# A two-layer decoder on one Trainium2 core: half-size parcels of filler in the stick-breaking mixer, one PSUM bank for two products of a down part, and weight parts behind the copy of u

## The chip, the cores and the metric

The kernel runs on one core of one Trainium2 chip. The metric is the device time of one execution in microseconds (us), as the median over runs. Times of single instructions come from one execution that the hardware profiler recorded. In what follows PE is TensorE (matrix products), PEld its weight load, ACT is ScalarE, DVE is VectorE, POOL is GpSimd and SP is SyncE, which issues nearly all transfers here. PSUM is the memory that PE writes its products to; it has eight banks, each of 512 fp32 columns on 128 partitions.

## The reference

The kernel computes two layers of a decoder for one sequence of 512 tokens with 1024 features. Each layer adds three things to the residual stream x: half a SwiGLU feed-forward (FFN), a mixer, and half a second FFN. The mixer of layer 0 is a gated linear attention (GLA), that of layer 1 a stick-breaking attention (SB).

```python
def swiglu(h, w_gate, w_up, w_down):
    return (jax.nn.silu(h @ w_gate) * (h @ w_up)) @ w_down

def sb_mixer(h, w_in, w_out):
    ...
        z = jnp.einsum('bhtd,bhsd->bhts', q_blk, k).astype(jnp.float32) * scale
        ...
        sp = jnp.where(mask, jax.nn.softplus(z), 0.0)
        rem = lax.cumsum(sp, axis=3, reverse=True) - sp
        weights = jnp.where(mask, jnp.exp(jax.nn.log_sigmoid(z) - rem), 0.0)
        return jnp.einsum('bhts,bhsd->bhtd', weights.astype(v.dtype), v)
    ...
    return o @ w_out

def reference(x, ...):
    for i in range(DEPTH):                                  # DEPTH = 2
        x = x + 0.5 * swiglu(rmsnorm(x, ffn1_norm[i]), ...)  # d_ff = 2816
        h = rmsnorm(x, mix_norm[i])
        y = gla_mixer(h, ...) if i % 2 == 0 else sb_mixer(h, ...)
        x = x + y
        x = x + 0.5 * swiglu(rmsnorm(x, ffn2_norm[i]), ...)
    return rmsnorm(x, final_norm)
```

## The kernel before

**Products.** Every large product is made of three: an operand is cut into a high part (a cast, `wh` or `xh`) and a low part (the difference, `wl` or `xl`), and PE adds high by high, low by high and high by low into one PSUM bank (`mm3`, line 68). Cutting a weight costs ACT the cast of line 129 and DVE the difference of line 130. x stays on chip, feature-major (`xs`, eight tiles of 128 features by 512 tokens).

**The queue of work.** All weight work is a list of entries in `feed` (line 140). An entry has weight units and a body, a generator that issues matmuls and yields between parcels. `Feed.start` (line 144) begins an entry: it cuts the units of this entry and of the next two, as long as these hold no more than four large units (1024 elements a partition), looks one entry further for the sums of weights, and issues the transfers of six entries. Within an engine the program order is what is written, but a scheduler places the engines' instructions by priority; `tc.issue_after(x)` puts what is issued under it behind x. `feed.step(n)` (line 161) runs n parcels. A mixer calls it between its own operations, so that PE has filler while ACT and DVE work on the attention.

**Sizes of parcels.** `feat` (line 192) makes 128 features for 512 tokens in 24 matmuls of 512 columns, in two parcels. `tok` (line 211) makes 256 features token-major in 96 matmuls of 256 columns, in four parcels. `back` makes the projection back into x, and `two_halves` (line 561) takes the first two `feat` entries of a phase in turn.

**PSUM.** `psum` (line 47) hands out the eight banks in the order of "aazzztto", or by a tag.

**The FFN.** Most gate and up products are made by `seven` (line 666): a product of 2 x 2 blocks with seven block products in place of eight, as in Strassen's and Winograd's schemes. It queues two entries. `body_1` takes three weight units (a block, `sums_12`, two blocks) and makes the first four block products with 256 columns each: w, q, w again, z; ACT copies the first w into z (line 718). `body_2` takes one unit (`sums_34`) and makes the other three: w (12 matmuls, operand `t_half(2)`), then the copy of w to u on ACT (`u3`, line 736), then q, then w. Its adds and gates are on DVE (lines 737, 740, 706).

**Down parts.** `down` (line 300) adds one part of the down projection into x, with 512 columns a matmul. For two of the six groups of each FFN, `seven_down` (line 336) does it with seven block products: its entries are again a `body_1` and a `body_2`, sixteen pairs of them in the kernel. In `body_1` each of the two q products (m = 0, 1; six matmuls of 256 columns each) takes a bank of its own, and an add into x (line 378) follows each product. w and z take two banks each as well, so that one `seven_down` holds six.

**The SB mixer.** `SB` (line 1257) queues the input projections as filler: for each of eight pairs of heads a q and a k `feat` entry (`pair`), and four `tok` entries for v (`vals`); the projection back follows. `evac_k` (line 1296) turns one product into the two heads' keys: a multiplication by the norm (`n`), then two casts to `kh` (one on ACT, one on DVE) and two operations for `kl` of each head. `run` (line 1394) goes over 17 iterations s. Iteration s makes the logits and running sums of head s (`weights_log`: z on PE; four ACT operations; scans on DVE; r on DVE, line 1352) and the transposes and exponentials of head s-1 (`weights`: `ps_T` on PE, `wt` on ACT, line 586); after each odd head `values` (line 1373) multiplies by v for a pair (`ps_oT`, line 1381). Pair p is needed by iteration 2p, the values of group c by the iteration that closes pair 2c. How many parcels of filler each iteration gets is written out by hand:

```python
                steps = [3] * 12 + [2, 1, 1, 2, 2]
```

Of the kernel before, what the change touches and what calls it, by code (L numbers as in the profile page):

```python
# [21 lines left out]
KD = D // P  # L22
# [10 lines left out]
def decoder(ctx: ExitStack, tc: tile.TileContext, a: dict, out: bass.AP):  # L33
# [60 lines left out]
    class Entry:  # L94
# [4 lines left out]
        def __init__(self, units, body, place=0, lead=False):  # L99
            self.units, self.body, self.W, self.place = units, body, None, place  # L100
            self.lead, self.views = lead, None

# [5 lines left out]

        def split(self):
            if self.W is None:  # L110
                self.W = []
                for r, (_, _, n, m) in zip(self.view(), self.units):
                    few = n * m < 1024
# [26 lines left out]
    class Feed:  # L140
# [3 lines left out]
        def start(self):  # L144
            i = self.pos
            self.pos += 1
            used = 0
            for e in self.q[i : i + 3]:
                used += sum(n * m >= 1024 for _, _, n, m in e.units)
                if used > 4:  # L150
                    break
                e.split()
            for e in self.q[i : i + 4]:
                e.view()
            for e in self.q[i : i + 6]:
                for u in e.units:
                    u[0].load()
            e = self.q[i]
            return e.body(e.W)

        def step(self, n=1, end=None):
            while n > 0:
                if self.cur is None:
                    if self.pos == end:
                        return
                    self.cur = self.start()
                if next(self.cur, self) is self:
                    self.cur = None
                else:
                    n -= 1  # L170
# [21 lines left out]
    def feat(ch, f, evac, tag=None, defer=None):  # L192


        def body(W):
            (wh, wl), = W
            ps = psum("ps_f", tag)
            for part in (range(0, KD // 2), range(KD // 2, KD)):
                for k in part:
# [11 lines left out]
    def tok(w, c0, evac, tag=None):  # L211
# [3 lines left out]
        def body(W):  # L215
            ps = None
            for i in range(NT):
# [4 lines left out]
                for k in range(KD):  # L222
                    wh, wl = W[k // 4]
                    mm(o, st["h"][k][:, s], wh[:, k % 4], k == 0, False)
                    mm(o, st["h"][k][:, s], wl[:, k % 4], False, False)
                    mm(o, st["l"][k][:, s], wh[:, k % 4], False, k == KD - 1)
                if i % 2:
                    evac(i - 1, ps[:, 0:256])
                    evac(i, o)
# [6 lines left out]
    def back(w, r0, nf, hs, scale, nxt, late=0, tags=(None,) * 8):  # L236


        for dh in range(2):
# [27 lines left out]
            if nf == KD and late:  # L267

                def body(W, prod=prod, done=done):
                    for ms in ((0, 1), (2, 3)):  # L270
                        for f in range(nf - late):
                            for m in ms:
                                prod(W, f // 2, f % 2, m, f)
                            if f % 2:
                                yield
                    for m in range(4):
                        for f in range(nf - late, nf):
                            prod(W, f // 2, f % 2, m, f)
                        done(m)
                        yield  # L280

                feed.q.append(Entry([u for _, u in units], body))
                continue
            for f0, u in units:

                def body(W, f0=f0, prod=prod, done=done):
                    if f0 + 2 < nf:
                        for kk in range(2):
                            for m in range(4):
                                prod(W, 0, kk, m, f0 + kk)  # L290
                            yield
                    else:
                        for m in range(4):
                            for kk in range(2):
                                prod(W, 0, kk, m, f0 + kk)
                            done(m)
                            yield

# [37 lines left out]
    def seven_down(pool, w, r0, hs, part):  # L336
# [43 lines left out]
        def body_1(W):  # L380
# [5 lines left out]
            for m in range(2):  # L386
# [3 lines left out]
                nc.scalar.copy(zs[m], ws[m])  # L390
            yield
            for m in range(2):
                qs.append(psum("ps_q")[:, 0:H])
                prod(qs[m], s, 0, m, "t1", True)
                add(m, 1, 1, qs[m])
# [11 lines left out]
        def body_2(W):  # L407
# [9 lines left out]
            for m in range(2):  # L417
                prod(qs[m], s, 2, m, "b22", False)
                add(m, 0, 1, qs[m])
            yield  # L420
# [40 lines left out]
    st = {}  # L461
# [99 lines left out]
    def two_halves(between=None):  # L561
# [3 lines left out]
        for i in range(3):  # L565
            for x in g:
                next(x, None)
            if i == 0 and between is not None:
# [20 lines left out]
    class FFN:  # L589
# [76 lines left out]
        def seven(self, ch, group=None):  # L666
# [63 lines left out]
            def body_2(W):  # L730
# [4 lines left out]
                u3 = self.tp.tile([P, H], F32, tag="c", bufs=1, name="u3")  # L735
                nc.scalar.copy(u3, w)  # L736
                nc.vector.tensor_tensor(out=o1[:, H:T], in0=u3, in1=o1[:, H:T], op=ALU.add)
# [34 lines left out]
            feed.q.append(entry)  # L772
            feed.q.append(Entry([(ch, sums_34, KD, P)], body_2, NEAR))

        def t_half(self, i, j):
# [481 lines left out]
    class SB:  # L1257
# [5 lines left out]
        def __init__(self, w_in, w_out, nxt):  # L1263
# [11 lines left out]
            pair(0), vals(0), pair(1), pair(2), vals(1), pair(3), pair(4), vals(2)  # L1275
            pair(5), pair(6), vals(3), pair(7)
            back(w_out, 0, KD, self.hs, 1.0, nxt, late=2, tags=("a", "a", "z", "z", "z", "t", "t", "o"))
# [116 lines left out]
        def run(self):  # L1394
            with ExitStack() as es:
# [17 lines left out]
                feed.step(4)  # L1413
                steps = [3] * 12 + [2, 1, 1, 2, 2]
                for s in range(17):
# [3 lines left out]
                    if s < 16:  # L1419
                        for i, _ in enumerate(self.weights_log(p, e)):  # L1420
                            if i == 1:
                                feed.step(1)
                                n -= 1
                    if s > 0:
                        for i, _ in enumerate(self.weights(q, f)):
                            if i < 2 and n > 0:
                                feed.step(1)
                                n -= 1
                        feed.step(n)
                        if f == 1:  # L1430
                            self.values(q)
                    else:
                        feed.step(n)
                feed.entries(self.end + 2 - feed.pos)
# [321 lines left out]
```

## Time and profile before

| | us |
|---|---|
| three runs | 1831.89, 1834.36, 1835.29 |
| their median | 1834.36 |
| the profiled execution | 1833.41 |
| its span | 1831.5 |

By the tiles' names and times the phases lie about so: first FFN 23 to 345 us, GLA mixer to 585, FFN to 915, FFN to 1250, SB mixer to 1475, last FFN to the end.

A row of the page's first section gives an engine's busy time, its share of the span and its count of instructions. Rows of groups name line, engine, operation, output and inputs, shapes and count; behind the bar stand the busy time in us, the mean of one in ns, and the idle time of the engine before them with what ended it. In a list of waits stand the waiting product, what it waited for, the total, the count and the longest. In a timeline stand start, duration, and in brackets the idle time before. Matmuls overlap, so their pace is read from start to start; a matmul's shown duration is longer than its share of PE.

### The profile page before, as it was taken

Reading aid. Unit: us, or ns where it says so; the run is one execution under the profiler, and the core shown is the slowest. Engines: PE = TensorE matmul, PEld = TensorE weight load, DVE = VectorE, ACT = ScalarE, POOL = GpSimd, SP = SyncE. Lnnn points to the kernel's source line nnn. Section 1 sums busy time; section 2 is a strip of 40 time slices with the busy share of each in tenths; the row PEclk is TensorE's granted clock in tenths of the full one; section 3 lists DMA queues with packets and bytes.
Section 4 is the critical chain, followed back from the end, with each engine's and each line's share of the span. In section 5 each row is a group of like instructions: output and inputs, shape, how many; then the busy total and the mean of one; then the engine's idle time right before and its main releaser. Section 6 shows DMA issues by size and latency. Waiting matters only on the chain.

```text
span 1831.5 us, 30847 instructions
## 1 busy us (share of the span) xinstructions
PE 1820.1 (99%) x12496; PEld 1657.0 (90%) x12496; DVE 1544.3 (84%) x2529; ACT 1058.7 (58%) x1856; POOL 8.8 (0%) x20
## 2 busy tenths in 40 slices
PE   9999999999999999999999999999999999999998
PEld 7999999889888899999889999998888788999997
DVE  8999798676787989889798988976878779898886
ACT  6556555544555556555555555555878755565554
POOL 0000000000000000000000000000000000000000
PEclk9999999999999999999999999999999999999999
DMA  5433333221123333333333333322222133233331
GB/s 163 137 115 106 104 116 117 79 70 55 62 69 115 93 115 100 120 104 104 99 98 115 93 115 116 104 82 81 70 70 64 64 92 115 93 116 104 104 121 53
DMA packets 177794, 179.22 MB, mean 98 GB/s; under 512 B 4146, under 2 KB 168292, under 8 KB 177652
## 3 DMA queue, kind: packets, MB, share of 16 engines
q1 hardware_dynamic: 176800, 175.91, 30.8%
q8 instruction: 98, 1.61, 0.4%
q0 software_dynamic: 608, 1.05, 0.2%
q14 instruction: 44, 0.36, 0.1%
q10 hardware_dynamic: 244, 0.29, 0.0%
HBM read 175.17 MB, written 2.10 MB: 97 GB/s over the span
## 4 chain that ended last, share of the span: by engine, by line
PE 94%; DVE 4%; ACT 1%; DMA 1%; issue 0%; SPq 0%; DVEq 0%; ACTq 0%
PE ps_w L693 21%; PE ps_f L66 18%; PE ps_d L66 16%; PE ps_q L693 10%; PE ps_z L693 5%; PE ps_t L66 5%; PE ps_w L372 4%; PE ps_b L66 4%; PE ps_q L372 2%; PE ps_S L66 1%; PE ps_z L1319 1%; PE ps_z L372 1%; PE ps_oT L1381 1%; DVE wl L130 1%; PE ps_bt L66 1%; PE ps_T L1366 1%
## 5 line engine op out<-in xcount | busy, mean ns | idle before, releaser
L130 DVE TENSOR_TENSOR wl<-raw,wh 128x512 fp32r<-128x512 f32 (+1 forms) x242 | 256.7, 1061 | 66.8 <-ACT wh L129 47.7
L129 ACT CAST wh<-raw 128x512 fp32r<-128x512 f32 (+1 forms) x242 | 223.5, 925 | 97.7 <-PE ps_f L66 32.8
L130 DVE TENSOR_TENSOR wl<-s,wh 128x1024 fp32r<-128x1024 f32 x176 | 214.6, 1220 | 46.9 <-PE ps_z L693 29.1
L129 ACT CAST wh<-s 128x1024 fp32r<-128x1024 f32 x176 | 184.2, 1047 | 109.5 <-DVE s L683 25.1
L693 PE MATMUL ps_w<-th,wh 128*128 128x256 f32 x864 | 239.5, 277 | 1.0 <-ACT u L736 0.9
L693 PE MATMUL ps_w<-tl,wh 128*128 128x256 f32 x864 | 238.7, 276 | 0.0
L693 PE MATMUL ps_w<-th,wl 128*128 128x256 f32 x864 | 238.7, 276 | 0.0
L66 PE MATMUL ps_f<-xh,wh 128*128 128x512 f32 x432 | 172.4, 399 | 0.0
L66 PE MATMUL ps_f<-xl,wh 128*128 128x512 f32 x432 | 169.3, 392 | 0.0
L66 PE MATMUL ps_f<-xh,wl 128*128 128x512 f32 x432 | 168.9, 391 | 0.0
L693 PEld LDWEIGHTS ps_w<-th,wh 128*128 128x128 f32 x864 | 162.4, 188 | 1.8 <-ACT u L736 1.3
L66 PE MATMUL ps_d<-hh,wl 128*128 128x512 f32 x416 | 162.2, 390 | 0.0
L66 PE MATMUL ps_d<-hh,wh 128*128 128x512 f32 x416 | 162.2, 390 | 0.0
L693 PEld LDWEIGHTS ps_w<-th,wl 128*128 128x128 f32 x864 | 162.2, 188 | 0.0
L693 PEld LDWEIGHTS ps_w<-tl,wh 128*128 128x128 f32 x864 | 162.2, 188 | 0.0
L66 PE MATMUL ps_d<-hl,wh 128*128 128x512 f32 x416 | 161.8, 389 | 0.0
L129 ACT CAST wh<-rawd 128x1024 fp32r<-128x1024 f32 (+1 forms) x100 | 82.9, 846 | 71.8 <-issue 31.8
L130 DVE TENSOR_TENSOR wl<-rawd,wh 128x1024 fp32r<-128x1024 f32 (+1 forms) x100 | 96.0, 963 | 16.4 <-PE ps_z L693 8.6
L327 DVE SCALAR_TENSOR_TENSOR x<-ps_d,x 128x512 f32<-128x512 f32 x120 | 81.2, 686 | 22.9 <-PE ps_d L66 22.5
L66 PEld LDWEIGHTS ps_f<-xl,wh 128*128 128x128 f32 x432 | 81.1, 188 | 17.3
L66 PEld LDWEIGHTS ps_f<-xh,wl 128*128 128x128 f32 x432 | 81.3, 188 | 15.7
L66 PEld LDWEIGHTS ps_f<-xh,wh 128*128 128x128 f32 x432 | 81.2, 188 | 15.3
(353 smaller groups left out, 5286.1 us busy)
## 6 DMA issues: line engine op xcount, KB each, us to landing
raw<-in_ffn_w_gate_dram SPq DMA_DIRECT2D x43, 1024.0 KB, 5.4
raw<-in_ffn_w_up_dram SPq DMA_DIRECT2D x43, 1024.0 KB, 5.4
rawd<-in_ffn_w_down_dram SPq DMA_DIRECT2D x84, 512.0 KB, 3.6
raw<-in_gla_w_in_dram SPq DMA_DIRECT2D x12, 1024.0 KB, 5.3
raw<-in_sb_w_in_dram SPq DMA_DIRECT2D x16, 512.0 KB, 3.8
raw<-in_gla_w_out_dram SPq DMA_DIRECT2D x4, 1024.0 KB, 4.9
raw<-in_sb_w_in_dram SPq DMA_DIRECT2D x4, 1024.0 KB, 5.2
raw<-in_sb_w_out_dram SPq DMA_DIRECT2D x4, 1024.0 KB, 5.0
```

What stands on the lines that cost most here:

```text
L66: st["pe"] = nc.tensor.matmul(ps, l, r, start=first, stop=last).ins
L129: st["cut"] = nc.scalar.copy(h[:, k], part).ins
L130: nc.vector.tensor_tensor(out=l[:, k], in0=part, in1=h[:, k].bitcast(F32), op=ALU.subtract)
L327: nc.vector.scalar_tensor_tensor(out=xs[k], in0=ps, scalar=0.5, in1=xs[k], op0=ALU.mult, op1=ALU.add)
L372: st["pe"] = nc.tensor.matmul(ps, l_, r_, start=first and c + n == 0, stop=c == 1 and n == 2, skip_group_check=True).ins
L693: st["pe"] = nc.tensor.matmul(o, l_, r_, start=first and j + n == 0, stop=j == 3 and n == 2, skip_group_check=True).ins
L1319: nc.tensor.matmul(o_, l_, r_, start=first, stop=last, skip_group_check=True)
L1366: nc.tensor.transpose(ps[:, c0 : c0 + P], ys[yb][:, yc + j * P : yc + (j + 1) * P], ident)
L1381: nc.tensor.matmul(po[e * 64 : e * 64 + 64, j * P : T], self.v[j][:, c : c + 64], self.wt[p, e][bk][:, c0 : c0 + n], start=j == 0, stop=j ...
```

## The change

Three things change; the instructions are the same in number on every engine.

*Half-size parcels.* `feat` yields four times in place of two, `tok` eight times in place of four, the projection back twice where it did once. `Feed.step(n)` now runs 2n of these half parcels (`halves`), so that the GLA mixer keeps its sizes. The SB mixer hands them out itself: 6 half parcels in the first three iterations and 5 in the other fourteen, 88 in all as before. In its list of entries the last pair of heads goes ahead of the last group of values.

*One bank for two products.* In `seven_down` both q products go to the two halves of one PSUM bank. Only the first sets the start flag, and both adds follow both products, in `body_1` and in `body_2`.

*Weight parts behind the copy of u.* The `body_2` entries of `seven` are marked `mid`. Where such an entry starts, and the next entry is a down part, and the one behind that is another `seven` entry (or a `seven_down`; both have the place `NEAR`), only the first unit of that last entry is cut at once. The others (the sums `s12` and the two blocks) are cut after the first chunk of `body_2`, and issued behind the copy of u.

```diff
--- before.py
+++ after.py
@@ -98,7 +98,7 @@
 
         def __init__(self, units, body, place=0, lead=False):
             self.units, self.body, self.W, self.place = units, body, None, place
-            self.lead, self.views = lead, None
+            self.lead, self.views, self.mid = lead, None, False
 
         def view(self):
 
@@ -106,10 +106,13 @@
                 self.views = [view(ch.load()) for ch, view, _, _ in self.units]
             return self.views
 
-        def split(self):
+        def split(self, count=None, after=None):
             if self.W is None:
                 self.W = []
-                for r, (_, _, n, m) in zip(self.view(), self.units):
+            done = len(self.W)
+            with tc.issue_after(after) if after is not None else ExitStack():
+                for r, (_, _, n, m) in list(zip(self.view(), self.units))[done:count]:
                     few = n * m < 1024
                     if few:
 
@@ -145,20 +148,35 @@
             i = self.pos
             self.pos += 1
             used = 0
+            hold = None
+            if self.q[i].mid and i + 2 < len(self.q) and self.q[i + 1].units[0][0].few and self.q[i + 2].place == NEAR:
+                hold = self.q[i + 2]
             for e in self.q[i : i + 3]:
                 used += sum(n * m >= 1024 for _, _, n, m in e.units)
                 if used > 4:
+                    hold = None
                     break
-                e.split()
+                e.split(1 if e is hold else None)
             for e in self.q[i : i + 4]:
                 e.view()
             for e in self.q[i : i + 6]:
                 for u in e.units:
                     u[0].load()
             e = self.q[i]
-            return e.body(e.W)
+            return e.body(e.W) if hold is None else self.held(e, hold)
+        @staticmethod
+        def held(e, hold):
+            for n, _ in enumerate(e.body(e.W)):
+                if n == 0:
+                    hold.split(None, st["u3"])
+                yield
 
         def step(self, n=1, end=None):
+            self.halves(2 * n, end)
+        def halves(self, n, end=None):
             while n > 0:
                 if self.cur is None:
                     if self.pos == end:
@@ -195,7 +213,7 @@
         def body(W):
             (wh, wl), = W
             ps = psum("ps_f", tag)
-            for part in (range(0, KD // 2), range(KD // 2, KD)):
+            for part in (range(u, u + KD // 4) for u in range(0, KD, KD // 4)):
                 for k in part:
                     mm3(ps, wh[:, k], wl[:, k], st["h"][k], st["l"][k], k == 0, k == KD - 1)
                 if part[-1] == KD - 1:
@@ -224,6 +242,8 @@
                     mm(o, st["h"][k][:, s], wh[:, k % 4], k == 0, False)
                     mm(o, st["h"][k][:, s], wl[:, k % 4], False, False)
                     mm(o, st["l"][k][:, s], wh[:, k % 4], False, k == KD - 1)
+                    if k == KD // 2 - 1:
+                        yield
                 if i % 2:
                     evac(i - 1, ps[:, 0:256])
                     evac(i, o)
@@ -271,12 +291,12 @@
                         for f in range(nf - late):
                             for m in ms:
                                 prod(W, f // 2, f % 2, m, f)
-                            if f % 2:
-                                yield
+                            yield
                     for m in range(4):
                         for f in range(nf - late, nf):
                             prod(W, f // 2, f % 2, m, f)
                         done(m)
+                        yield
                         yield
 
                 feed.q.append(Entry([u for _, u in units], body))
@@ -289,11 +309,13 @@
                             for m in range(4):
                                 prod(W, 0, kk, m, f0 + kk)
                             yield
+                            yield
                     else:
                         for m in range(4):
                             for kk in range(2):
                                 prod(W, 0, kk, m, f0 + kk)
                             done(m)
+                            yield
                             yield
 
                 feed.q.append(Entry([u], body))
@@ -389,9 +411,12 @@
                 zs.append(psum("ps_z")[:, 0:H])
                 nc.scalar.copy(zs[m], ws[m])
             yield
+            ps = psum("ps_q")
             for m in range(2):
-                qs.append(psum("ps_q")[:, 0:H])
-                prod(qs[m], s, 0, m, "t1", True)
+                qs.append(ps[:, m * H : (m + 1) * H])
+                prod(qs[m], s, 0, m, "t1", m == 0)
+            for m in range(2):
                 add(m, 1, 1, qs[m])
             yield
             for m in range(2):
@@ -416,6 +441,7 @@
             yield
             for m in range(2):
                 prod(qs[m], s, 2, m, "b22", False)
+            for m in range(2):
                 add(m, 0, 1, qs[m])
             yield
             for m in range(2):
@@ -564,7 +590,7 @@
         g = [feed.start(), feed.start()]
         for i in range(3):
             for x in g:
-                next(x, None)
+                next(x, None), next(x, None)
             if i == 0 and between is not None:
                 between()
 
@@ -733,7 +759,7 @@
                 o0, o1 = v["o"]
                 prod(w, s, 0, lambda j: self.t_half(2, j), first=False)
                 u3 = self.tp.tile([P, H], F32, tag="c", bufs=1, name="u3")
-                nc.scalar.copy(u3, w)
+                st["u3"] = nc.scalar.copy(u3, w).ins
                 nc.vector.tensor_tensor(out=o1[:, H:T], in0=u3, in1=o1[:, H:T], op=ALU.add)
                 yield
                 prod(q, s, 4, half(4, 1), first=False)
@@ -771,6 +797,7 @@
             entry = Entry(units, body_1, NEAR, lead)
             feed.q.append(entry)
             feed.q.append(Entry([(ch, sums_34, KD, P)], body_2, NEAR))
+            feed.q[-1].mid = True
 
         def t_half(self, i, j):
 
@@ -1273,7 +1300,7 @@
                 tok(w_in, 2 * D + c * 256, lambda i, ps: self.evac_v(c, i, ps), "z" if c == 0 else "a")
 
             pair(0), vals(0), pair(1), pair(2), vals(1), pair(3), pair(4), vals(2)
-            pair(5), pair(6), vals(3), pair(7)
+            pair(5), pair(6), pair(7), vals(3)
             back(w_out, 0, KD, self.hs, 1.0, nxt, late=2, tags=("a", "a", "z", "z", "z", "t", "t", "o"))
 
         def evac_v(self, c, i, ps):
@@ -1411,7 +1438,8 @@
                 exp_ln_tables(st["sqrt"])
                 flush(self.defer)
                 feed.step(4)
-                steps = [3] * 12 + [2, 1, 1, 2, 2]
+                steps = [6] * 3 + [5] * 14
                 for s in range(17):
                     p, e = divmod(s, 2)
                     q, f = divmod(s - 1, 2)
@@ -1419,18 +1447,19 @@
                     if s < 16:
                         for i, _ in enumerate(self.weights_log(p, e)):
                             if i == 1:
-                                feed.step(1)
-                                n -= 1
+                                feed.halves(2)
+                                n -= 2
                     if s > 0:
                         for i, _ in enumerate(self.weights(q, f)):
-                            if i < 2 and n > 0:
-                                feed.step(1)
-                                n -= 1
-                        feed.step(n)
+                            if i < 2:
+                                k = min(n, n % 2 if i == 0 and n % 2 else 2)
+                                feed.halves(k)
+                                n -= k
+                        feed.halves(n)
                         if f == 1:
                             self.values(q)
                     else:
-                        feed.step(n)
+                        feed.halves(n)
                 feed.entries(self.end + 2 - feed.pos)
```

## The prediction

> **What bounds the kernel now.** I read the page first: its busy times and the granted clock.
>
> ```profile
> span 1831.5 us, 30847 instructions
> ...
> PE 1820.1 (99%) x12496; PEld 1657.0 (90%) x12496; DVE 1544.3 (84%) x2529; ACT 1058.7 (58%) x1856; POOL 8.8 (0%) x20
> ...
> PEclk9999999999999999999999999999999999999999
> ```
>
> TensorE (PE) is busy for all but 11.4 us of the span and its clock is granted in full. The change issues the same instructions as before on every engine, so it can save only time in which PE stands still or refills its pipeline. Next I asked which waits PE has; the columns are the total in us, the count and the longest.
>
> ```profile
> PE ps_q L372 <- DVE o L706: 1.1, 4, 0.3
> ...
> PE ps_w L693 <- ACT u L736: 0.9, 2, 0.7
> ...
> PE ps_z L1319 <- DVE r L1352: 0.4, 2, 0.2
> ...
> PE ps_oT L1381 <- ACT wt L586: 0.2, 1, 0.2
> ```
>
> Each of the three parts of the change meets one of these: the bank of the products of a down part (`ps_q` at line 372), the copy of u (line 736), and the mixer's filler (the last two). The waits of the first 23 us, left out here, are out of its reach. So the profile itself bounds the visible gain at 2.6 us; what a wait costs beyond its idle time comes next. Last I looked at the load of the other engines by stage: an FFN stretch, the mixer's regular part, and its tail.
>
> ```profile
> 1025.00:1050.00 25.00, 25.00 (x223) 25.00 (x223) 24.88 (x43) 15.69 (x28) 0.00 (x0) 1.00 0.37 116
> 1275.00:1425.00 150.00, 150.00 (x930) 122.81 (x928) 120.84 (x175) 124.29 (x249) 0.00 (x0) 1.00 0.22 68
> 1425.00:1450.00 25.00, 24.38 (x132) 16.90 (x131) 20.15 (x31) 22.08 (x49) 0.00 (x0) 1.00 0.13 43
> ```
>
> After the stretch's length stand the busy times of PE, its weight load, VectorE (DVE) and ScalarE (ACT). In the FFN, DVE is as full as PE; in the mixer ACT and DVE stand at 83% and 81%.
>
> **Part 1, one bank for two products.** The timeline of PE around one of the four waits, then around a place that the list of waits does not show:
>
> ```profile
> 254.20 0.28 PE L372 MATMUL ps_q<-hh,wl 128*128 128x256 f32 x1
> 254.31 0.28 PE L372 MATMUL ps_q<-hl,wh 128*128 128x256 f32 x1
> 254.88 0.38 PE L372 MATMUL ps_q<-hh,wh 128*128 128x256 f32 x1 [0.29 <-DVE o L706]
> 255.10 0.29 PE L372 MATMUL ps_q<-hh,wl 128*128 128x256 f32 x1
> ...
> 851.58 0.28 PE L372 MATMUL ps_q<-hl,wh 128*128 128x256 f32 x1
> 851.80 0.38 PE L372 MATMUL ps_q<-hh,wh 128*128 128x256 f32 x1
> ```
>
> Matmuls of this size start 0.113 us apart. Here the second q product starts 0.57 after its predecessor, and its next one 0.22 later: 0.46 + 0.11, so 0.56 us where the list shows 0.29 of idle time. A shown wait costs about twice its idle time. What it waits for is a gate of the unit before, which reads the bank that the product takes:
>
> ```profile
> 254.41 0.42 DVE L706 TENSOR_TENSOR o<-ps_w,o 128x256 f32<-128x256 f32 x1
> ```
>
> The gate ends at 254.83. With both q products in one bank the second takes no new bank, and a down part needs five of the eight instead of six; in the built order the gate's bank is reused after about 5 us of matmuls instead of 2.15. The four waits go: 4 x 0.56 = 2.24 us. At 851.80, and alike at 1762, 0.21 each goes too: 2.65 us in all.
>
> The price: the add of the first product (line 378) now follows both products, and PE may write the bank again (`b22`) only behind both adds.
>
> ```profile
> 139.35 0.75 DVE L378 SCALAR_TENSOR_TENSOR x<-ps_q,x 128x256 f32<-128x256 f32 x2
> ...
> 137.78 0.28 PE L372 MATMUL ps_q<-hl,wh 128*128 128x256 f32 x1
> ...
> 141.98 0.28 PE L372 MATMUL ps_q<-hh,wh 128*128 128x256 f32 x1
> ```
>
> The second product's last matmul starts at 137.78, the two adds end at 140.10 and the bank is written again at 141.98: 1.9 us of cover (PE's ws, zs and t3 products). The adds are behind both products already, since DVE's queue is late, so I take 0. The Trainium skill's page "PSUM — Partial Sum Buffer", section "PSUM bank collisions raise a hardware error", speaks against sharing: two engines may not touch one bank at once, so an add cannot run beside a product in the other half. By that rule the first add could move by six matmuls at most, an estimate of 0.68 us; the rows above show more cover than that.
>
> **Part 2, the weight parts behind the copy of u.** PE and then ACT around the longer of the two waits, and PE at the other:
>
> ```profile
> 661.36 0.28 PE L693 MATMUL ps_q<-nl,wh 128*128 128x256 f32 x1
> 662.29 0.39 PE L693 MATMUL ps_w<-th,wh 128*128 128x256 f32 x1 [0.66 <-ACT u L736]
> 662.52 0.28 PE L693 MATMUL ps_w<-th,wl 128*128 128x256 f32 x1
> ...
> 660.92 1.05 ACT L129 CAST wh<-s 128x1024 fp32r<-128x1024 f32 x1 [1.59 <-DVE s L677]
> 661.88 0.36 ACT L736 COPY u<-ps_w 128x256 f32<-128x256 f32 x1
> ...
> 1572.14 0.28 PE L693 MATMUL ps_q<-nl,wh 128*128 128x256 f32 x1
> 1572.66 0.38 PE L693 MATMUL ps_w<-th,wh 128*128 128x256 f32 x1 [0.24 <-ACT u L736]
> ```
>
> ACT's queue is in order. The cast of the down part's sums waits for DVE (the s of line 677) until 660.92 and holds the copy up until 661.88. PE's next product should have started at 661.47; it starts at 662.29 and refills for 0.11: 0.93 us. At 1572.66 it is 0.41 + 0.11 = 0.52. Both lie ahead of a down part, where the change puts the cast and its difference behind the copy: 1.45 us saved. The two moved pieces cost PE nothing if they are ready in time:
>
> ```profile
> L130 DVE TENSOR_TENSOR wl<-s,wh 128x1024 fp32r<-128x1024 f32 x176 | 214.6, 1220 | 46.9 <-PE ps_z L693 29.1
> L129 ACT CAST wh<-s 128x1024 fp32r<-128x1024 f32 x176 | 184.2, 1047 | 109.5 <-DVE s L683 25.1
> ```
>
> Cast and difference take 1.05 + 1.22 = 2.3 us. Between the copy and the first product of s lie two products of u's unit (24 matmuls, 2.7 us), the earlier down part (24 at twice the width, 5.4 us) and the products of a11 (12, 1.4 us): 9.5 us. What waits behind the copy's chunk on DVE is the rest of that unit's adds, which move at most by these 2.3 us. I take 0; bounds -0.3 to +1 us, since DVE is full there. A DMA that the swap of the mixer's parts moves three issues later on SP stays two raw buffers ahead: 0.
>
> **Part 3, half parcels.** The mixer's filler by groups, in 1275 to 1425:
>
> ```profile
> L66 PE MATMUL ps_f<-xh,wh 128*128 128x512 f32 x102 | 42.2, 414 | 0.0
> ...
> L66 PE MATMUL ps_t<-wh,xh 128*128 128x256 f32 x96 | 27.7, 288 | 0.0
> ...
> 1435.80 0.48 PE L66 MATMUL ps_b<-oh,wh 128*128 128x512 f32 x1
> ```
>
> A half parcel is 6 matmuls of 512 columns or 12 of 256: 12 x 0.113 = 1.36 us. With three matmuls a step the rows give 306 / 6 + 288 / 12 = 75 half parcels, at 6 an iteration 12.5 iterations of 12.0 us: 8.16 filler, 3.84 its own. The old plan gives the last five iterations 4, 2, 2, 4, 4 half parcels; the new one gives 6 to the first three and 5 to the fourteen others, which makes an iteration 10.6 us. So the regular part is thinned to feed the tail. In the tail the two last waits of the list (0.6 us idle) cost about twice that, 1.2, with 0.3 of slower starts that show no idle time; and six single matmuls that cut the filler at 0.09 each (the row at 1435.80 lasts 0.48 against some 0.39): 2.0 us to gain at most. Against it: the built order resumes filler 55 times instead of 49, +0.5; pair 5 is due at 52 half parcels and now has 53 done instead of 60. Its keys go through these:
>
> ```profile
> L1304 DVE CAST kh<-n 64x512 fp32r<-64x512 f32 x12 | 5.1, 422 | 0.3
> ...
> L1305 DVE TENSOR_TENSOR kl<-n,kh 64x512 fp32r<-64x512 f32 x12 | 8.2, 681 | 0.2
> ```
>
> Two casts and two differences are 2.2 us against the 1.36 of the one spare parcel and the matmuls between: a stall of 0 to 1.5, I take 0.2. A `ps_b` bank is wanted 2.1 us after its last writer, 0 to 0.5, I take 0.25. Net -2.0 + 0.5 + 0.2 + 0.25 = -1.0, bounds -2.0 to +2.0.
>
> **The sum.** -2.65 - 1.45 - 1.0 = -5.1 us. The profiled execution took 1833.41 (1.9 around its span), which gives 1828.3. The median of the three runs is 1834.36, their mean 1833.85; I add the mean's 0.44: 1828.8.
>
> **The rivals.**
> - *The mixer gives back what it gains.* For it: DVE and ACT above 80%, pair 5 with one parcel to spare. Against: PE has no wait at all in 1275 to 1425. Part 3 at 0 to +2: 1829.8 to 1831.8, say 1831.
> - *Slower: ACT becomes the bound of the five-parcel iterations.* ACT is busy 124.29 / 12.5 = 9.94 us an iteration and idle 2.06. One parcel fewer takes at least its share of the weight casts off it:
>
> ```profile
> L129 ACT CAST wh<-raw 128x1024 fp32r<-128x1024 f32 x19 | 20.2, 1064 | 9.8 <-DMA raw<-in_sb_w_in_dram 5.6 <-PE ps_f L66 4.1
> ```
>
> 20.2 / 75 = 0.27, leaving 9.67 in 10.64. If its idle time is latency that stays, an iteration takes 11.7, 1.09 more, 14 times 15.3: 1828.8 + 15.3 - 0.5, about 1843. It decides from 0.66 an iteration (slower than the median by 0.2%). Against: the old tail has iterations of 2 and 4 parcels at ACT 22.08 of 25 and lost only some 1.5 us over five.
> - *The shared bank stalls PE.* If DVE were so late that the 1.9 us of cover were gone, each of 16 down parts would lose up to the 0.68 us: +10.9, near 1840. Against: the adds' rows above.
> - *The FFN waits only move.* The first q product may meet the late gate, and the copy of z (line 718) the late cast in place of u. Then parts 1 and 2 bring a third, 1.4: with part 3, 1831.5. Against: the bank's reuse distance.
>
> **Chances.** Forecast 0.60 (own range 1825.8 to 1831.5, by part 3's bounds and the spread of 3.4 us between runs); mixer gives back 0.20; ACT-bound 0.09; shared bank 0.03; waits move 0.08. 0.2% (3.7 us, about what can be told from no change) puts the bounds at 1830.7 and 1838.0. Faster: 0.54 + 0.06 + 0.02 = 0.62; slower: 0.09 + 0.03 and 0.01 of the first rival, 0.13; the same 0.25. The range 1825.5 to 1834.5 leaves out most of the slow cases.
>
> **What would show it.** Right: `ps_q` at line 372 and `ps_w` behind the copy of u are gone from PE's waits, and the mixer's tail shows PE at 25 of 25. Wrong: new waits of PE at line 1319 or 1381 before 1425, `ps_q` at 372 behind line 378, or `ps_q` on the late cast of s. A slower pace of matmuls with no waits would be no effect of these steps.

## The result, and the profile after

| | before | after |
|---|---|---|
| median of 22 runs | 1835.26 | 1837.61 |
| lowest to highest | 1831.89 to 1836.35 | 1833.16 to 1841.04 |
| the profiled execution | 1833.41 | 1836.06 |

The ratio is 1.0016, with a 95% interval from 1.0010 to 1.0022: the changed kernel is a little slower, by 2.35 us. 1828.8 had been forecast, with 1834.5 as the upper end. It also scatters more, over 7.9 us against 4.5.

First the waits of PE in the changed kernel, with the total in us, the count and the longest, below those of the start:

```profile
PE ps_z L1346 <- ACT kh L1330: 0.5, 1, 0.5
...
PE ps_z L1346 <- DVE kl L1333: 0.2, 1, 0.2
```

The waits on the gate (`ps_q`), on the copy of u and on the mixer's tail are gone, as forecast; in 1425 to 1450 PE is busy for 24.94 of 25 us, where it was for 24.38. In their place stand the keys of pair 5 and one wait of 0.3 us in the first FFN. By this list the kernel should be faster. The list hides what was lost, because it counts idle time that the modelled ends of the matmuls leave. The starts of the matmuls show it. PE in the changed kernel, in the first down part with seven products, behind the products of q and behind those of z:

```profile
138.18 0.28 PE L394 MATMUL ps_q<-hh,wl 128*128 128x256 f32 x1
138.29 0.28 PE L394 MATMUL ps_q<-hl,wh 128*128 128x256 f32 x1
138.68 0.38 PE L394 MATMUL ps_w<-hh,wh 128*128 128x256 f32 x1
138.90 0.28 PE L394 MATMUL ps_w<-hh,wl 128*128 128x256 f32 x1
...
141.39 0.28 PE L394 MATMUL ps_z<-hl,wh 128*128 128x256 f32 x1
141.74 0.39 PE L394 MATMUL ps_w<-nh,wh 128*128 128x256 f32 x1
141.97 0.28 PE L394 MATMUL ps_w<-nh,wl 128*128 128x256 f32 x1
```

The pace is 0.113. At 138.68 PE starts 0.27 late and then loses another 0.11 up to its next start (the refill), at 141.74 it is 0.24 late and refills again. No idle time stands in brackets, since it is shorter than a matmul's modelled overlap. Such a pair stands at eight of the sixteen down parts, always in the first part of a group. The sixteen late starts and their refills sum to 5.3 us. None was there before.

Who is late is seen on ACT and DVE of the changed kernel, ahead of the first late start and ahead of the second:

```profile
136.79 0.62 ACT L817 CAST hh<-o 128x512 fp32r<-128x512 f32 x1 [1.21 <-DVE o L732]
137.31 1.05 ACT L132 CAST wh<-s 128x1024 fp32r<-128x1024 f32 x1
138.27 0.63 ACT L412 COPY ps_z<-ps_w 128x256 f32<-128x256 f32 x2
...
136.33 0.42 DVE L732 TENSOR_TENSOR o<-o,o 128x256 f32<-128x256 f32 x1
...
140.61 0.75 DVE L400 SCALAR_TENSOR_TENSOR x<-ps_q,x 128x256 f32<-128x256 f32 x2
141.28 0.74 DVE L400 SCALAR_TENSOR_TENSOR x<-ps_w,x 128x256 f32<-128x256 f32 x2
```

The same in the kernel before, with the two starts of PE:

```profile
135.06 0.42 DVE L706 TENSOR_TENSOR o<-o,o 128x256 f32<-128x256 f32 x1
...
135.52 0.63 ACT L790 CAST hh<-o 128x512 fp32r<-128x512 f32 x1 [0.45 <-DVE o L706]
136.05 1.04 ACT L129 CAST wh<-s 128x1024 fp32r<-128x1024 f32 x1
137.00 0.63 ACT L390 COPY ps_z<-ps_w 128x256 f32<-128x256 f32 x2
...
137.90 0.28 PE L372 MATMUL ps_w<-hh,wh 128*128 128x256 f32 x1
...
140.01 0.75 DVE L378 SCALAR_TENSOR_TENSOR x<-ps_w,x 128x256 f32<-128x256 f32 x2
...
140.62 0.28 PE L372 MATMUL ps_w<-nh,wh 128*128 128x256 f32 x1
```

After the change, the gate on DVE ends at 136.75. The cast of the hidden tile (`hh`) waits for it, the weight cast queues behind that, and the copy of w to z behind both: its first half ends at 138.63, and PE may write w again at 138.68. Before, ACT did the same three in the same order, and its first half copy was done at 137.36, half a microsecond ahead of PE. PE begins the products of q 0.51 later in this trace (137.05 against 136.54), the gate ends 1.27 later: 0.76 later against PE. The first add of w starts at 141.28 and takes 0.41 of the row's 0.74 for two; it lets go the bank that PE takes at 141.74. Before, that add came 0.2 us ahead of PE (140.01 to 140.43, PE at 140.62). So DVE runs some 0.8 us further behind PE than it did. It fell behind 29 us earlier, where DVE of the changed kernel, and then of the kernel before, stand ahead of a down part:

```profile
107.30 0.42 DVE L732 TENSOR_TENSOR o<-ps_z,o 128x256 f32<-128x256 f32 x1 [2.43 <-PE ps_z L719]
108.20 0.42 DVE L818 TENSOR_TENSOR nl<-o,nh 128x256 fp32r<-128x256 f32 x1 [0.47 <-ACT nh L817]
109.12 0.42 DVE L763 TENSOR_TENSOR o<-u,o 128x256 f32<-128x256 f32 x1 [0.49 <-ACT u L762]
109.58 0.43 DVE L732 TENSOR_TENSOR o<-o,o 128x256 f32<-128x256 f32 x1
110.07 1.23 DVE L133 TENSOR_TENSOR wl<-s,wh 128x1024 fp32r<-128x1024 f32 x1
```

```profile
106.78 1.23 DVE L130 TENSOR_TENSOR wl<-s,wh 128x1024 fp32r<-128x1024 f32 x1 [2.42 <-PE ps_z L693]
107.93 0.42 DVE L706 TENSOR_TENSOR o<-ps_z,o 128x256 f32<-128x256 f32 x1
108.56 0.43 DVE L737 TENSOR_TENSOR o<-u,o 128x256 f32<-128x256 f32 x1 [0.21 <-ACT u L736]
```

Before, the difference of the down part's next unit (`wl<-s`, 1.23 us) filled DVE's time while PE was still at the product of w. With its cast put behind the copy of u, DVE has nothing to do there: it stands still for 0.47 and 0.49 us where it stood for 0.21, and does the difference later. At equal points of PE's order, DVE's work done is 0.79 us less than before from here to the down part at 138. It had no idle time in between to make up for it.

A third thing is in the trace. In one FFN stretch, before and then after:

```profile
725.00:750.00 25.00, 25.00 (x223) 25.00 (x222) 23.52 (x40) 14.99 (x30) 0.00 (x0) 1.00 0.36 115
```

```profile
725.00:750.00 25.00, 25.00 (x215) 25.00 (x214) 22.82 (x37) 16.27 (x33) 0.00 (x0) 1.00 0.40 128
```

PE is busy throughout in both, and its granted clock is 1.00 in both, yet it gets through eight matmuls fewer. It goes at 0.118 us a matmul in place of 0.113, and began to at a late start, 708.26:

```profile
708.26 0.39 PE L394 MATMUL ps_w<-hh,wh 128*128 128x256 f32 x1
708.48 0.28 PE L394 MATMUL ps_w<-hh,wl 128*128 128x256 f32 x1
708.60 0.28 PE L394 MATMUL ps_w<-hl,wh 128*128 128x256 f32 x1
708.72 0.28 PE L394 MATMUL ps_w<-hh,wh 128*128 128x256 f32 x1
708.83 0.28 PE L394 MATMUL ps_w<-hh,wl 128*128 128x256 f32 x1
708.95 0.28 PE L394 MATMUL ps_w<-hl,wh 128*128 128x256 f32 x1
709.07 0.28 PE L394 MATMUL ps_w<-hh,wh 128*128 128x256 f32 x1
```

So the FFNs' matmuls of 256 columns can be sorted by the time from start to start: a late start is one of over 0.126 us, a slow one is of 0.1155 to 0.126, and what each has over 0.1133 is summed. That gives two numbers for a trace, used for all kernels below (the last down part, `ps_bt`, is left out). Before they are 5.1 us late and 2.2 slow, after 6.3 and 5.6. With the mixer (from the last of its sums, `ps_st`, to the last product of its projection) at 231.6 us against 233.9, the two profiled executions are accounted for: +1.2 late, +3.5 slow, -2.2 mixer, and some +0.1 in the start and the GLA mixer, against a difference of 2.65 between them. The slow term differs from execution to execution, as the runs below show, so this sum holds for these two executions alone.

### The profile page after: what moved, and what is told of

The parts are those of the page before. It is cut to its first block, busy times and chain, and to the rows that moved or that the text cites. A ratio compares the mean times of both kernels' runs of the same rounds, so it can differ in the third digit from the quotient of the medians.

```text
span 1834.2 us, 30800 instructions
## 1 busy us (share of the span) xinstructions
PE 1823.2 (99%) x12496; PEld 1658.9 (90%) x12496; DVE 1544.0 (84%) x2529; ACT 1064.6 (58%) x1856; POOL 8.8 (0%) x20
## 4 chain that ended last, share of the span: by engine, by line
PE 82%; DVE 12%; ACT 3%; issue 1%; DMA 1%; SPq 0%; DVEq 0%; ACTq 0%
PE ps_w L719 17%; PE ps_f L66 17%; PE ps_d L66 14%; PE ps_q L719 8%; PE ps_t L66 5%; DVE wl L133 4%; PE ps_z L719 4%; PE ps_w L394 4%; PE ps_b L66 4%; PE ps_q L394 2%; PE ps_S L66 1%; PE ps_z L1346 1%; ACT wh L132 1%; PE ps_oT L1408 1%; DMA raw<-in_ffn_w_up_dram 1%
```

## The experiments

Three theories were set against each other. A: the late cut of weight parts (the third part of the change) makes DVE idle in a stretch where it has no time to spare, and PE waits for it later. B: the shared bank makes PE wait for the adds. C: the slow stretches come by chance and are all there is. The first four kernels ran on one chip, where the kernel before had a median of 1832.74 us.

**Without the late cut.** Half parcels and shared bank stay.

```diff
-            feed.q[-1].mid = True
```

> The changed kernel without its third part: all weight parts are cut at once again; half parcels and the shared bank stay. Theory A (the late cut leaves DVE idle ahead of a down part, DVE is full behind it, so its gates come late and PE waits at line 394): the sixteen late starts of ps_w that stand in the changed kernel's trace (5.3 us with their refills) go, with them most of the slow stretches of matmuls that follow some of them (about 3 us), and 1.5 us of waits on the copy of u come back: 1830 to 1832 us, below the kernel before. Theory B (the shared bank makes PE wait for the adds): the sixteen late starts stay, 1836 to 1839. Theory C (the slow stretches come by chance and are all there is): about the changed kernel's 1837.6, the late starts gone or not.

1827.30 us, ratio 0.9970 (0.9958 to 0.9981). Late 1.0 us, slow 2.4. The late starts behind q and z are gone; PE at the first place:

```profile
139.01 0.28 PE L394 MATMUL ps_q<-hl,wh 128*128 128x256 f32 x1
139.12 0.28 PE L394 MATMUL ps_w<-hh,wh 128*128 128x256 f32 x1
```

That is 5.4 us below before. Theory A holds and B falls, with one miss: no wait on the copy of u came back. The kernel with the shared bank alone, below, shows why.

**The late cut alone**, on the kernel before: `hold`, `held`, `split(count, after)` and `mid`, with the old parcels and two banks.

> The kernel before with the third part alone. Theory A: the late starts of ps_w behind the products of q appear, 1.5 us of waits on the copy of u and no bank wait go: 1838 to 1841 us against 1835.3 before. Theory B: only the waits on u go, 1833 to 1834. Theory C: within 1 us of before.

1839.34 us, ratio 1.0037 (1.0024 to 1.0049). That is 6.6 us above before, more than the 2.7 to 5.7 that were expected. Late 8.4, slow 7.6. Eight of the changed kernel's sixteen late starts are there; at the four places where the kernel before waited for a bank, that wait has grown. Its waits, and DVE at one of them:

```profile
PE ps_q L390 <- DVE o L725: 3.8, 4, 1.0
```

```profile
257.56 0.44 DVE L725 TENSOR_TENSOR o<-ps_w,o 128x256 f32<-128x256 f32 x1
```

The gate that held the bank until 254.83 before now ends at 258.00, 0.6 us later against PE: PE starts 1.03 late in place of 0.45, and 1.16 late at the three other places. This is theory A's DVE backlog again, seen through another wait.

**The shared bank alone.**

```diff
+            ps = psum("ps_q")
             for m in range(2):
-                qs.append(psum("ps_q")[:, 0:H])
-                prod(qs[m], s, 0, m, "t1", True)
-                add(m, 1, 1, qs[m])
+                qs.append(ps[:, m * H : (m + 1) * H])
+                prod(qs[m], s, 0, m, "t1", m == 0)
+            for m in range(2):
+                add(m, 1, 1, qs[m])
...
                 prod(qs[m], s, 2, m, "b22", False)
+            for m in range(2):
                 add(m, 0, 1, qs[m])
```

> The kernel before with the shared bank alone. Theory A: the bank's four waits and two short ones go and nothing comes for them: 1831.5 to 1833 us against 1835.3. Theory B: the sixteen late starts of ps_w appear: 1837 to 1840.

1828.57 us, ratio 0.9978 (0.9968 to 0.9988). Late 1.2, slow 0.2. All bank waits are gone, no late start behind the adds has come, and both waits on the copy of u are gone as well, although nothing was done to them. ACT at the first of these places, in this kernel:

```profile
660.39 0.37 ACT L739 COPY u<-ps_w 128x256 f32<-128x256 f32 x1 [1.03 <-PE ps_w L696]
660.94 1.05 ACT L129 CAST wh<-s 128x1024 fp32r<-128x1024 f32 x1 [0.18 <-DVE s L680]
```

The copy, which stood behind that cast at 661.88 before, now stands ahead of it. The scheduler had put the two the other way round; why it did was not tried. With the half parcels alone, below, both waits on u are still there (PE 0.83 and 0.82 late). So the second part of the gain came with the first, and the code written for it was not needed.

**The half parcels alone**, with the new order of the last pair and the last values.

> The kernel before with the half parcels and the new order of the last pair and the last values alone. From the changed kernel's trace, whose mixer is 2.2 us shorter than the mixer before: all theories 1832.5 to 1834 us against 1835.3, no late start of ps_w in a down part, and the four bank waits still there.

1830.43 us, ratio 0.9989 (0.9980 to 0.9998). Late 4.9, slow 1.6, the mixer 231.6 us. The time lies below the expected 1832.5 to 1834 because the kernel before was faster on this chip too; against it the gain is 2.3 us, within the 1.3 to 2.8 that were expected. The four bank waits are still there.

**DVE's time or ACT's order?** The late cut changes both. Here the cut is at once again, and DVE gets two needless operations where the late cut used to act. This kernel ran on a second chip (before: 1835.06), with the changed kernel and the last kernel of this section.

```diff
-                e.split(1 if e is hold else None)
+                e.split()
...
-            return e.body(e.W) if hold is None else self.held(e, hold)
+            st["pad"] = hold is not None and len(hold.units) > 1
+            return e.body(e.W)
...
                 nc.vector.tensor_tensor(out=o1[:, H:T], in0=u3, in1=o1[:, H:T], op=ALU.add)
+                if st["pad"]:
+                    for _ in range(2):
+                        nc.vector.tensor_tensor(out=u3, in0=u3, in1=u3, op=ALU.max)
```

> The changed kernel without the late cut, but with two needless DVE operations of 128x256 (some 0.67 us together) behind the add of u at the same twenty places at which the late cut acts: ACT's order stays as without the late cut, only DVE loses time. Theory A (what the late cut costs is DVE time in a stretch in which DVE has none to spare): late starts of PE in the down parts come back, 4 to 9 us above no_hold. Rival (it is ACT's order, the cast behind the copy, that delays the copies of the down part): at most 1 us above no_hold.

1834.35 us, ratio 0.9993 (0.9984 to 1.0001), that is 3 to 4 us above the kernel without the late cut, which lay at 0.9970 on its chip and at 0.9976 on a third; a little less than expected. Late 4.7. PE in this kernel:

```profile
141.01 0.28 PE L395 MATMUL ps_z<-hl,wh 128*128 128x256 f32 x1
141.34 0.38 PE L395 MATMUL ps_w<-nh,wh 128*128 128x256 f32 x1
```

The late start behind z is back at all eight places; the one behind q is next to nothing (0.02). So DVE's time explains one of the two, and the other stayed open until three operations were tried, on the third chip (before: 1835.18):

> As dve_pad, with three needless operations (1.0 us of DVE at each of the twenty places instead of 0.67). With two, the late start behind the products of z stood at all eight places (0.22 us) and the one behind the products of q was almost nothing (0.02). If the second too is only DVE's backlog, it now grows to 0.25 to 0.4 and the first to 0.3 or more: 3 to 7 us above dve_pad's distance from before, that is 2 to 6 us above before. If it needs ACT's order as well, the start behind q stays below 0.1.

1836.69 us, ratio 1.0009 (1.0000 to 1.0017), 1.5 us above before where 2 to 6 were expected. Late 6.4, as in the changed kernel.

```profile
139.36 0.28 PE L395 MATMUL ps_q<-hl,wh 128*128 128x256 f32 x1
139.88 0.38 PE L395 MATMUL ps_w<-hh,wh 128*128 128x256 f32 x1 [0.24 <-ACT ps_z L413]
```

The start behind q is now 0.40 late at four places and 0.15 at the others, without any change that was made to ACT's order by hand. Behind z it stayed at 0.14 to 0.23, below what was expected. One microsecond of DVE at twenty places gives this kernel the late starts that the late cut gives it. The rival, ACT's order, is not needed for them: ahead of each of the sixteen pairs of copies of w to z, the three instructions of ACT are the same and in the same order in the kernels before and after, without the late cut, with it alone, and with either padding. The padded kernel's median is still 3.2 us below the changed kernel's on this chip (1839.86); what makes up the difference no trace shows.

**The changed kernel again**, on the second and the third chip.

> The changed kernel itself once more, so that it stands beside the next three on one chip and a second trace shows which of its slow stretches of matmuls stay in place. 2 to 3 us above the kernel before; the sixteen late starts of ps_w at the same places and of the same size, the slow stretches (118 ns a matmul in place of 113) at partly other places.

> The changed kernel a third time, beside the three below on one chip: 0 to 2.5 us above the kernel before, with the same sixteen late starts and between 3 and 6 us of slow stretches in its trace.

1835.36 us against 1835.06, ratio 1.0003 (0.9995 to 1.0012); and 1839.86 against 1835.18, ratio 1.0021 (1.0012 to 1.0029). Both miss what was expected: 0.3 us above before in place of 2 to 3, and 4.7 in place of 0 to 2.5, with 0.8 us of slow stretches where 3 to 6 were expected. The late starts are 6.1 and 6.4 us, at the same places as in the first trace (6.3). The slow stretches are 4.1 and 0.8 us, at other places, and the profiled executions follow them: 1836.06 with 5.6 us slow, 1834.44 with 4.1, 1832.17 with 0.8. The last is the fastest of its twelve runs; the others (1838 to 1841) left no trace.

**The two best again**, on the third chip beside it.

> The changed kernel without the late cut, again, now beside the changed kernel: 5 to 6 us below before, 5 to 8 us below the changed kernel.

> The kernel before with the shared bank alone, again: 3.5 to 4.5 us below before, and 1 to 2.5 us above the changed kernel without the late cut, which also has the mixer's 2.2 us. If slow stretches of matmuls differ by chance, up to 1.5 us more or less.

1830.91 us, ratio 0.9976 (0.9966 to 0.9986), and 1834.10 us, ratio 0.9994 (0.9985 to 1.0003). The kernel without the late cut is faster than the kernel before on both chips, and 9.0 us faster than the changed kernel on the third. It gained 4.3 on before where 5 to 6 were expected, and 9.0 on the changed kernel where 5 to 8 were; 5.4 of the 9.0 are the late starts of the two traces. The shared bank alone lost most of its gain: 1.1 us below before where 3.5 to 4.5 were expected, and no longer clear of no change, though its late starts are the same (1.2). A stretch of its first trace and the same stretch of its second:

```profile
725.00:750.00 25.00, 25.00 (x223) 25.00 (x222) 23.74 (x43) 15.19 (x28) 0.00 (x0) 1.00 0.33 107
```

```profile
725.00:750.00 25.00, 25.00 (x213) 25.00 (x214) 23.65 (x39) 14.79 (x29) 0.00 (x0) 1.00 0.33 108
```

This is one program, with the same data, on two chips. The second execution has 5.8 us of slow matmuls, the first 0.2, and they took 1833.18 and 1827.87 us. In the second PE falls into the slow pace here:

```profile
724.71 0.28 PE L696 MATMUL ps_q<-tl,wh 128*128 128x256 f32 x1
724.84 0.39 PE L696 MATMUL ps_w<-th,wh 128*128 128x256 f32 x1
725.06 0.28 PE L696 MATMUL ps_w<-th,wl 128*128 128x256 f32 x1
725.18 0.28 PE L696 MATMUL ps_w<-tl,wh 128*128 128x256 f32 x1
725.30 0.28 PE L696 MATMUL ps_w<-th,wh 128*128 128x256 f32 x1
```

The start at 724.84 is 0.017 us late, and PE does not come back to 0.113 behind it.

**More filler early.** Without the late cut, and with the half parcels dealt out so that pair 5 has two more done when it is due (on the second chip).

```diff
-                steps = [6] * 3 + [5] * 14
+                steps = [6] * 5 + [5] * 10 + [4] * 2
```

> The changed kernel without the late cut, with half parcels handed out as five times 6, ten times 5, twice 4, so that pair 5 has 55 half parcels done instead of 53 when it is due. If the two late starts at line 1345 (1.1 us together in no_hold) are pair 5's keys coming late, they go: 0.7 to 1.2 us below no_hold, less what two tail iterations of 4 give back (0 to 0.5). If they come from something else in that iteration, no change.

1831.22 us, ratio 0.9975 (0.9963 to 0.9986). The waits for pair 5's keys are gone, but the mixer takes 231.5 us as with them: other waits took their place. One wait is new in this kernel, in the last FFN, which the edit does not touch; below it stand the new one in the mixer, and DVE ahead of the first:

```profile
PE ps_w L719 <- ACT ps_z L744: 1.8, 1, 1.8
...
PE ps_b L66 <- DVE r L1378: 0.3, 1, 0.3
...
1626.19 0.69 DVE L702 TENSOR_TENSOR s<-raw 128x512 f32<-128x512 f32 x1 [1.87 <-DMA raw<-in_ffn_w_gate_dram]
```

There DVE waited 1.87 us for a block of weights: its transfer took 7.88 us from issue to landing, where the same block took 5.57 in the kernel without the late cut, and DVE's order is otherwise the same. PE then started 1.95 late. One trace cannot say whether the edit or chance made that transfer slow. So the gain expected of this edit is not shown; the mixer, where it should stand, is no shorter.

## Why the prediction was wrong

- *Part 1, one bank, -2.65 us:* right, and its price of 0 too. Late starts fell from 5.1 to 1.2 us with this part alone, where parts 1 and 2 together had been forecast at -4.1; the medians fell by 4.2 us on one chip and by 1.1 on another. The rival of the shared bank is out. By the Trainium skill's page "PSUM — Partial Sum Buffer" (section "PSUM bank collisions raise a hardware error"), two engines may not access one bank at once, so that the adds stand behind both products. PE waits for none of these adds in the trace of the shared bank alone. What the prediction did not look at is the next cover: the adds of q have 1.9 us, but the add of w stands next in DVE's queue and has 0.2.
- *Part 2, -1.45 us, "The two moved pieces cost PE nothing if they are ready in time":* this step failed. In place of a gain of 1.45, the late cut cost 6.6 us by itself (1839.34 against 1832.74) and 9.0 in the changed kernel (1839.86 against 1830.91). The gain came without it, by the scheduler's order. PE shows no wait for the moved pieces, so the 9.5 us of margin sufficed. But I asked when the moved work is due and not what DVE does in the time that it leaves empty. Moving it made DVE idle, 0.79 us at the place shown, in a stretch where I had read that DVE is as full as PE. The 5.3 us of late starts in the first part of each group's down part follow from it, as padding DVE by 1.0 us at the same places confirms (late starts of 6.4 us in both). The "-0.3 to +1 us" I gave as bounds were too narrow: the cut acts at twenty places, and 20 times the 0.79 us seen since, some 16, would have been the upper bound. The rival that came nearest was that the FFN's waits only move, but they moved by DVE's lost time and not by the ways that it gave.
- *Part 3, -1.0 us:* right in sign, mis-sized. The mixer gained 2.2 us in every trace with half parcels, just beyond the bound of -2.0. Pair 5's keys do come late, as the deadline said: PE starts 0.76 and 0.37 us late for them, where I took 0.2 from 0 to 1.5. If the other costs were as I took them, the tail gave more than the 2.0 I allowed; which of its waits did was not tried. ACT did not become the bound.
- *The slow pace:* the prediction set a slower pace of matmuls with no waits aside, as no effect of these steps. It changes from execution to execution by as much as the forecast gain, so theory C is right in this much. Whether new late starts bring more of it is not shown: the six traces with the late cut or the padding have 0.8 to 7.6 us of it, the seven others 0.2 to 5.8. That it makes up what the late starts leave of the 9.0 us is likely, but the slower runs left no trace.

Without part 2, the sum would have been -3.65 for parts 1 and 3 with no wait on u counted, or -5.1 with it; measured were -5.4 (1827.30 against 1832.74) and -4.3 (1830.91 against 1835.18). That they lie so close is in part luck, since part 3 brought twice its term and the slow pace alone moves an execution by some 5 us.

## What to carry to other kernels

Before work is moved later on an engine that is full, ask what the engine does in the gap that it leaves: if nothing, that time is lost, and it comes back as a wait at the next place with little cover, here 29 us later and on another engine. Where a scheduler orders the queues, take one wait away and look at the others again before they get code of their own. And read PE's starts, not only its list of waits: sixteen starts of 0.14 to 0.28 us late were 5.3 us with their refills and stood in no list.

## What the runs showed of the hardware

A late start of PE among matmuls of 128x256 costs its delay and 0.11 us at the next matmul. Beyond that PE may go on at 0.118 us a matmul in place of 0.113, with a granted clock of 1.00 throughout. Take as slow a stretch between two late starts, or up to the end of a run of 256-column products, whose starts are on average over 0.116 us apart. In the FFNs of the thirteen traces there are 50 of these, 49 of them behind one of 235 late starts (starts over 0.126 us after the one before; a refill counts with the start ahead of it). The fiftieth, in the second trace of the kernel without the late cut, set in at 812.27 us with a start only 0.005 late. 33 lasted until the run of 256-column products ended, 17 until another late start. The same program had 0.2 us of it in one execution and 5.8 in another on another chip, and the executions differed by 5.3. What makes one late start tip over and another not was not tried.
